# Resuming the pieces of GLA, S5 and mLSTM heads by stated waiting times, in an order pinned on TensorE and DVE

## The chip, the cores and the metric

The kernel runs on one core of a Trainium2 chip. The metric is device time in microseconds, from the start of an execution to its end; 0.2% of it is 3.5 us. The engines are TensorE (PE, with its weight loads as PEld), VectorE (DVE), ScalarE (ACT), GpSimd (POOL) and SyncE (SP), which issues the DMAs. Each works through its own queue in order and waits on semaphores.

## The reference

One layer of a hybrid model on a sequence of 1024 positions with 1024 channels: a mixer of three branches (512 channels each), then a feed-forward block with a convolution, each between two RMS norms. Cut to the mixer's inner parts, which the change touches:

```python
z = u @ w_in                          # u = rms_norm(x); queries, keys, values, gates of all branches
# GLA, 4 heads of 128: decay by log_sigmoid gates, in 16 chunks of 64
b = cumsum(log_a); q_dec = q * exp(b); k_inv = k * exp(-b)
kv = einsum(k * exp(b_last - b), v);  state = dec * state + kv       # over the chunks
o = q_dec @ s_prev + tril(q_dec @ k_inv.T) @ v;  o = rms_norm(o) * silu(r)
# S5, 32 groups of 16 channels, 64 complex states each
x[t] = ab * x[t-1] + bb @ u[t];  y = Re(c @ x) + d * u
# mLSTM, 4 heads of 128: conv + silu on q and k, stabilised gates, in 16 chunks of 64
c_new = sc * c + (w * k).T @ v;  qk = (q @ k.T) * exp(log_w - m)
hid = (s_inter * q @ c_prev + qk @ v) / max(abs(den), exp(-m));  hid = sigmoid(o) * hid
```

The rest of the layer (gates of the branches, their projections, `w_out`, the feed-forward block) is the same before and after.

## The kernel before, in words

All matmuls of weights run on fp32 values that are split into a high and a low part, three products for each step of 128 rows: high by high, high by low, low by high. `split` makes the two parts (ACT copies the high one at L88, DVE subtracts at L89). The first phase of the kernel, up to about 640 us, computes `z`. `chan_major` gives 128 channels for all positions in 48 matmuls of 512 columns (L126) into a PSUM tile `z` of two banks; `tok_mm` gives 128 positions for 256 channels in 24 matmuls (L184). There are two such `z` tiles, three single banks `m` (`bank`), and one bank `q` (`bank2`) for S5. In SBUF the S5 work has nine buffers of 128x512 (`q4`), the GLA and mLSTM work has fourteen of 128x1024 (`g`).

Beside these projections, on the same TensorE, run the pieces of the three branches. They are Python generators, and a `yield` ends a piece:

- `gla_gates` (one z tile, L332; then L337 to L356 on DVE and ACT) makes the decays of a head; `gla_inner` does the head: transposes of the decayed keys (L368), masked scores (L374, L375), chunk products (L384) and the decay chain of the states on DVE (L394, 15 steps), values (L400), the read-out (L410, added at L412), squares on POOL (L413), the norm (L415 to L417) and transposes out (L423, L425). The main program multiplies the decays by the projections at L890, L891 and L894.
- `s5_set`, eight times after `s5_base`: the set's input and its tables on POOL (L723 to L727, L735 to L737), two transposes (L742, L746), the response `kt` (L752, L753) which eight DMAs turn into the Toeplitz tile `tt`; the angles of the rotation through POOL, DVE and ACT (L767, L768, sine at L773, L774, cosine L776); `bv` times `ut` (L781); the rotation on DVE (L789) with eight scans (L799); then `ut` times `tt` (L812, copied out by ACT at L813), the states times `ca` (L816, added at L818), and, after every second set, transposes of `y` (L825).
- `ml_gates` and `ml_inner`: transposes of the keys (L552), scores (L559), states (L568, L571), read-out (L579 to L592), transposes out (L597). Convolution and SiLU of q and k (`conv_silu2`) are ACT L525, three DVE L527, ACT L530, DVE L531.

The list `running` holds the open generators; `advance()` steps each of them by one piece. It is called after a whole `chan_major` and after every fourth `tok_mm`; in the GLA and mLSTM loops `midway` also steps the S5 generator in the middle of a `chan_major`, six times in ten. This is the order in which the program is written. A scheduler then sets each engine's queue: among the instructions that are ready by its own cost model it takes the earliest written.

Of the kernel before, what the change touches and what calls it, by code (L numbers as in the profile page):

```python
# [32 lines left out]
def hybrid_layer(ctx: ExitStack, tc: tile.TileContext, a, out, dbg=None):  # L33
# [53 lines left out]
    def split(hi, lo, src):  # L87
        return (ordered("act", act.copy(hi, src)),  # L88
                ordered("dve", dve.tensor_tensor(lo, src, hi.bitcast(F32), op=ALU.subtract)))  # L89

# [26 lines left out]
    def chan_major(wt, i, xh, xl, ps=None, ns=(0, 1)):  # L117
# [14 lines left out]
    midway = []  # L132
# [7 lines left out]
    RATE = 0.6  # L140
# [38 lines left out]
    def tok_mm(wt, i, lhs, put, c0, to=None):  # L179
        hi, lo = wt  # L180
        ps = big()[:, 0, 0:hi.shape[2]] if to is None else to([128, hi.shape[2]])
        for k in range(8):
            for p, (l, r) in enumerate(((0, hi), (1, hi), (0, lo))):
                pe.matmul(ps, lhs(l, k, i), r[:, k, :],  # L184
                          start=(k == 0 and p == 0), stop=(k == 7 and p == 2))
        put(i, c0, ps)

# [141 lines left out]
    def gla_gates(h):  # L329
        ps = big()  # L330
        for n in range(2):
            pe.matmul(ps[:, n, :], wg[:, h * 128:(h + 1) * 128], lrx[:, n * 512:(n + 1) * 512],  # L332
                      start=True, stop=True)
        z = flat(ps)
        bias = cols[:, 40 + h:41 + h]
        ax, mn, b = g([128, S]), g([128, S]), g([128, S])
        dve.tensor_scalar(mn, z, bias, 0.0, op0=ALU.add, op1=ALU.min)  # L337
        dve.scalar_tensor_tensor(out=ax, in0=mn, scalar=2.0, in1=z, op0=ALU.mult, op1=ALU.subtract)
# [12 lines left out]
        return ax, b, mn, dec  # L351
# [7 lines left out]
    def gla_inner(h, E, r2):  # L359
        qd, ki, kd, dec = E  # L360
        vt = g([128, 8, 128])
        sync.dma_start(vt, v_dram[0][:, :, h * 128:(h + 1) * 128].rearrange("i p e -> p i e"))
        kt = g([128, 8, 128])
        for hf in range(2):
# [4 lines left out]
            act.copy(kt[:, hf * 4:hf * 4 + 4, :], ps)  # L369
        for hf in range(2):  # L370
# [5 lines left out]
        yield  # L376
        st = [g([128, 8, 128]) for _ in range(2)]
        pool.memset(st[0][:, 0, :], 0.0)
        for o in range(2):
# [22 lines left out]
        yield  # L402
        yield
        for hf in range(2):
# [8 lines left out]
            pool.tensor_tensor(sq, oo, oo, op=ALU.mult)  # L413
            ssq = small.tile([128, 4], F32, tag="ssq4", name="ssq4")
            dve.tensor_reduce(ssq, sq, axis=AX.X, op=ALU.add)  # L415
            rs = rstd_of(ssq, 4, DH)
            dve.tensor_tensor(oo, oo, rs.unsqueeze(2).to_broadcast([128, 4, 128]), op=ALU.mult)  # L417
        yield
        yield
# [24 lines left out]
    def ml_gates():  # L444
# [21 lines left out]
        yield  # L466
# [9 lines left out]
        yield  # L476
# [6 lines left out]
        yield  # L483
# [12 lines left out]
        yield  # L496
# [10 lines left out]
        yield  # L507
# [35 lines left out]
    def ml_inner(h, wm, qm, km, tm):  # L543
# [4 lines left out]
        for e in range(2):  # L548
            ps = bank([128, 4, 128])
            for q in range(4):  # L550
# [3 lines left out]
                              kwx[:, h, e * 4:e * 4 + 4].unsqueeze(2).to_broadcast([128, 4, 128]), op=ALU.mult)  # L554
        for e in range(2):
# [6 lines left out]
        yield  # L562
# [10 lines left out]
        yield  # L573
        nn = g([128, 8, 129])
        for j0, n in ((0, 3), (3, 3), (6, 2)):
# [8 lines left out]
            dve.tensor_tensor(dst, dst, pa[:, 0:n, :], op=ALU.add)  # L584
        rd = small.tile([128, 8], F32, tag="rd", name="rd")
# [7 lines left out]
        yield  # L593
        for e in range(2):
# [4 lines left out]
            dve.scalar_tensor_tensor(out=tm[0][:, t], in0=tm[0][:, t], scalar=1.0,  # L599
                                     in1=po.rearrange("p a b -> p (a b)"), op0=ALU.add, op1=ALU.mult)  # L600
        sync.dma_start(o_dram[2][h], tm[0])
# [99 lines left out]

    def s5_set(s):
# [11 lines left out]
        bst = s5p.tile([128, 2, 4, 16], F32, tag="bst", name="bst", bufs=1)  # L714
        for i, nm, p0 in ((0, "s5_b_re", 0), (0, "s5_b_im", 64), (1, "s5_b_im", 0), (1, "s5_b_re", 64)):
            sync.dma_start(bst[p0:p0 + 64, i], a[nm][0, gs].rearrange("g p h -> p g h"))
        cl = s5p.tile([64, 3, 64], F32, tag="cl", name="cl", bufs=1)
        for i, nm in ((0, "s5_c_re"), (1, "s5_c_im"), (2, "s5_c_re")):
            sync.dma_start(cl[:, i, :], a[nm][0, gs].rearrange("g h p -> (g h) p"))
# [7 lines left out]
        pool.tensor_copy(zr_, zt.rearrange("p j (g h) -> p g j h", h=16)[:, :, ::-1, :])  # L727
        ps = bank2([128, 2, 64])
# [9 lines left out]
        yield  # L738
# [8 lines left out]
        act.copy(ut, ps)  # L747
        kt = s5p.tile([16, 4, 15, 16], F32, tag="kt", name="kt", bufs=1)
# [28 lines left out]
        yield  # L777
# [26 lines left out]
        yield  # L804
        yield
        if s % 2 == 0:
            ysp.append(s5p.tile([128, 8, 128], F32, tag="ys", name="ys", bufs=1))
        ys = ysp[-1]
        dst = ys[:, :, c0:c0 + 64].rearrange("p j (g h) -> p g j h", h=16)
        ps = bank2(sq_)  # L810
        for q in range(4):
            pe.matmul(ps[:, q, :], ut[:, q, :], tt[:, q, :], start=True, stop=True)  # L812
        act.copy(dst, ps.rearrange("p q (j h) -> p q j h", h=16))  # L813
# [5 lines left out]
        if s % 2 == 0:  # L819
            return  # L820
        yield
        for e in range(2):
            ps = bank2(sq_)
            for q in range(4):
                pe.transpose(ps[:, q, :], ys[:, e * 4 + q, :], ident)  # L825
            yt = q4(sq_)
            act.activation(yt, ps, AF.Gelu_apprx_tanh)
            sync.dma_start(y_dram[s // 2][:, e * 512:(e + 1) * 512], yt.rearrange("p a b -> p (a b)"))

    ysp = []  # L830

    def s5_all():
        s5_base()
        yield
        for s in range(8):
            while s // 4 not in su_done:
                yield
            yield from s5_set(s)
            yield

    running = []
    credit = [0.0]

    def advance():
# [732 lines left out]
```

## Time and profile before

| | |
|---|---|
| median of 3 runs | 1745.9 us (1744.11 to 1747.18) |
| profiled execution, time | 1745.36 us |
| its span | 1743.6 us, so 1.76 us lie around it |
| granted TensorE clock, mean | 0.994 |
| PE, PEld busy | 1689.5 us (97%), 1412.1 us (81%) |
| DVE, ACT, POOL busy | 1151.8 us (66%), 646.8 us (37%), 398.1 us (23%) |

The span runs from the first to the last instruction. Busy shares are means over stages with different limits, and matmuls are pipelined, so the mean length of a matmul in a group is longer than the distance between two starts. A wait is the idle time in front of an instruction, put down to the engine and line whose semaphore came last. An idle engine matters only where TensorE waits for it in the end.

### The profile page before, as it was taken

Reading aid. Unit: us, or ns where it says so; the run is one execution under the profiler, and the core shown is the slowest. Engines: PE = TensorE matmul, PEld = TensorE weight load, DVE = VectorE, ACT = ScalarE, POOL = GpSimd, SP = SyncE. Lnnn points to the kernel's source line nnn. Section 1 sums busy time; section 2 is a strip of 40 time slices with the busy share of each in tenths; the row PEclk is TensorE's granted clock in tenths of the full one; section 3 lists DMA queues with packets and bytes.
Section 4 is the critical chain, followed back from the end, with each engine's and each line's share of the span. In section 5 each row is a group of like instructions: output and inputs, shape, how many; then the busy total and the mean of one; then the engine's idle time right before and its main releaser. Section 6 shows DMA issues by size and latency. Waiting matters only on the chain. (4 is left out here: it accounts for less than half of the span.)

```text
span 1743.6 us, 21877 instructions
## 1 busy us (share of the span) xinstructions
PE 1689.5 (97%) x8556; PEld 1412.1 (81%) x8556; DVE 1151.8 (66%) x1462; ACT 646.8 (37%) x940; POOL 398.1 (23%) x437
## 2 busy tenths in 40 slices
PE   6999998999999999999899999999999999999997
PEld 6997877897888888888688788788888888888886
DVE  4426677536667675444745654967777787669987
ACT  4544533333443223333510233433333333344343
POOL 1163243333334012222000011022322332101021
PEclk9999999999999999999899999999999999999999
DMA  6242131333141322434674643222232223483161
GB/s 205 68 113 60 43 88 34 92 91 89 23 133 49 97 85 85 127 115 145 222 249 144 217 142 125 73 73 82 76 90 79 85 73 97 169 283 127 55 218 54
DMA packets 196440, 195.10 MB, mean 112 GB/s; under 512 B 29208, under 2 KB 154305, under 8 KB 196337
## 3 DMA queue, kind: packets, MB, share of 16 engines
q1 hardware_dynamic: 195456, 190.56, 34.9%
q0 software_dynamic: 880, 3.15, 0.5%
q8 instruction: 67, 1.10, 0.3%
q14 instruction: 37, 0.30, 0.1%
HBM read 143.32 MB, written 48.25 MB: 110 GB/s over the span
## 5 line engine op out<-in xcount | busy, mean ns | idle before, releaser
L89 DVE TENSOR_TENSOR lo<-raw,hi 128x512 fp32r<-128x512 f32 (+3 forms) x163 | 174.7, 1091 | 132.0 <-ACT hi L88 129.3
L88 ACT CAST hi<-raw 128x512 fp32r<-128x512 f32 (+3 forms) x163 | 130.2, 833 | 283.1 <-PE z L126 122.0
L983 POOL TENSOR_TENSOR raw<-raw 128x512 f32<-128x512 f32 x28 | 39.5, 1412 | 472.4 <-DVE lo L89 472.4
L126 PE MATMUL z<-ohl,hi 128*128 128x512 f32 x448 | 123.3, 398 | 6.1 <-ACT ohl L1098 6.1
L126 PEld LDWEIGHTS z<-ohl,hi 128*128 128x128 f32 x448 | 85.5, 191 | 26.1 <-ACT ohl L1098 6.5
L68 POOL TENSOR_SCALAR rstd<-ssq 128x1 f32<-128x1 f32 (+1 forms) x32 | 9.3, 292 | 316.4 <-ACT x L1262 262.5
L126 PE MATMUL z<-u0h,hi 128*128 128x512 f32 x240 | 79.5, 408 | 1.4 <-DVE g L894 1.4
L126 PE MATMUL z<-u0h,lo 128*128 128x512 f32 x240 | 77.0, 398 | 0.0
L126 PE MATMUL z<-u0l,hi 128*128 128x512 f32 x240 | 76.5, 398 | 0.0
L126 PE MATMUL z<-u1h,hi 128*128 128x512 f32 x240 | 75.4, 395 | 0.0
L126 PE MATMUL z<-u1h,lo 128*128 128x512 f32 x240 | 75.0, 392 | 0.0
L126 PE MATMUL z<-u1l,hi 128*128 128x512 f32 x240 | 74.9, 393 | 0.0
L126 PE MATMUL z<-ohl,lo 128*128 128x512 f32 x224 | 70.2, 396 | 0.0
L1303 DVE SCALAR_TENSOR_TENSOR cv<-u,fcol,cv 128x1023 f32<-128x1023 f32 (+1 forms) x38 | 48.7, 1280 | 23.9 <-ACT cv L1301 23.9
L89 DVE TENSOR_TENSOR xl<-raw,xh 128x512 fp32r<-128x512 f32 x57 | 51.8, 935 | 11.2 <-ACT xh L88 8.3
L1301 ACT ACTIVATE cv<-u,fcol 128x1024 f32<-128x1024 f32 x19 | 23.6, 1244 | 89.9 <-DVE u L1001 89.9
L789 DVE TENSOR_TENSOR q<-q,q 128x512 f32<-128x512 f32 x72 | 49.5, 714 | 8.7 <-PE q L812 8.3
L126 PEld LDWEIGHTS z<-u0h,lo 128*128 128x128 f32 x240 | 45.3, 190 | 9.7 <-issue 0.2
L126 PEld LDWEIGHTS z<-u1h,lo 128*128 128x128 f32 x240 | 45.1, 188 | 9.8
L126 PEld LDWEIGHTS z<-u1l,hi 128*128 128x128 f32 x240 | 44.9, 188 | 9.9 <-issue 0.2
L126 PEld LDWEIGHTS z<-u0l,hi 128*128 128x128 f32 x240 | 44.8, 189 | 9.6 <-issue 0.4
L126 PEld LDWEIGHTS z<-u1h,hi 128*128 128x128 f32 x240 | 44.5, 188 | 9.3
(561 smaller groups left out, 5006.0 us busy)
## 6 DMA issues: line engine op xcount, KB each, us to landing
raw<-in_w_in_dram SPq DMA_DIRECT2D x48, 512.0 KB, 5.3
pt<-gate SPq DMA_DIRECT2D x24, 512.0 KB, 3.3
raw<-in_ffn_w_up_dram SPq DMA_DIRECT2D x22, 512.0 KB, 4.0
raw<-in_ffn_w_gate_dram SPq DMA_DIRECT2D x22, 512.0 KB, 5.3
h<-cv SPq DMA_DIRECT2D x21, 512.0 KB, 2.6
bx<-in_ffn_w_down_dram SPq DMA_DIRECT2D x15, 512.0 KB, 4.4
by<-in_ffn_w_down_dram SPq DMA_DIRECT2D x15, 512.0 KB, 5.1
gate<-u SPq DMA_DIRECT2D x11, 512.0 KB, 3.0
```

What stands on the lines that cost most here:

```text
L68: pool.tensor_scalar(r, ssq, 1.0 / width, EPS, op0=ALU.mult, op1=ALU.add)
L88: return (ordered("act", act.copy(hi, src)), ordered("dve", dve.tensor_tensor(lo, src, hi.bitcast(F32), op=ALU.subtract)))
L89: ordered("dve", dve.tensor_tensor(lo, src, hi.bitcast(F32), op=ALU.subtract)))
L126: pe.matmul(ps[:, n, :], l[:, k, c], r(k, n), start=(k == 0 and p == 0), stop=(k == nk - 1 and p == 2))
L789: dve.tensor_tensor(o, x, y, op=op)
L983: pool.tensor_tensor(a22, a21, a22, op=ALU.add)
L1301: first = act.activation(cv, src, AF.Identity, scale=fcol[:, 44 + f:45 + f], bias=fcol[:, 66 + f:67 + f])
L1303: ins = dve.scalar_tensor_tensor(out=cv[:, k:], in0=src[:, 0:S - k], scalar=fcol[:, (2 - k) * 22 + f:(2 - k) * 22 + f + 1], in1=cv[:, k:], ...
```

## The change

`advance`, `midway`, `extra` and `pump` go. In their place stands a list `turns` of generators with a due time each. `tick` is called after every six matmuls of `chan_major` (with 1.37 us, two halves) and halfway and at the end of each `tok_mm` (with 1.45 us each); it adds its time to a clock of the program and resumes the one generator that is longest overdue. A generator yields the time that it wants to wait before its next piece. `note` adds, at each resumption, a dependency without a semaphore from the first TensorE and the first DVE instruction of the piece to the newest instruction written before on that engine (splits of weights excepted), so that the scheduler can't put the piece ahead of it.

Beside this: `gla_gates` is a generator with two `m` banks in halves of 512 columns, no longer one z tile; the squares go from POOL to ACT; the product `ut` times `tt` stands before `bv` times `ut`; `s5_load` issues the loads of the next set after the rotation; the transposes of `y` are a generator of their own; `s5_all` starts ahead of the S5 input; `ml_inner` starts with the keys' convolution and takes q and o from a list when they are there.

```diff
-            if k == 3 and midway:
-                midway[0]()
+            tick(6 * len(ns) * 0.114)
...
+    def note(first=None):
+        traced = nc.cur_bb.bb.instructions
+        bound, work = set(), 0.0
+        for ins in traced[seen[0]:]:
+            e = ins.engine
+            if e == mybir.EngineType.PE:
+                work += 0.13
+            if e not in (mybir.EngineType.PE, mybir.EngineType.DVE):
+                continue
+            if first is not None and e not in bound and e in newest:
+                bound.add(e)
+                tc.add_manual_dep(ins, newest[e],
+                                  mybir.DependencyInfo(mybir.DependencyClass.NoSync, mybir.DependencyReason.DATA),
+                                  reason="turn")
+            if ins.name not in free_:
+                newest[e] = ins.name
...
+    def resume(turn_):
+        note()
+        try:
+            wait = next(turn_[1])
+        except StopIteration:
+            turns.remove(turn_)
+            wait = 0.0
+        now[0] += note(turn_)
+        turn_[0] = now[0] + wait
...
+    def tick(us):
+        now[0] += us
+        due = [t for t in turns if t[0] <= now[0]]
+        if due:
+            resume(min(due, key=lambda t: t[0]))
...
-        ps = big()
-        for n in range(2):
-            pe.matmul(ps[:, n, :], wg[:, h * 128:(h + 1) * 128], lrx[:, n * 512:(n + 1) * 512],
+        for n in range(2):
+            t = slice(n * 512, (n + 1) * 512)
+            z = bank([128, 512])
+            pe.matmul(z, wg[:, h * 128:(h + 1) * 128], lrx[:, t], start=True, stop=True)
...
-            pool.tensor_tensor(sq, oo, oo, op=ALU.mult)
+            act.activation(sq, oo, AF.Square)
+        yield 2.5
...
-        yield
+        yield 8.0
+        if s % 2 == 0:
+            ysp.append(s5p.tile([128, 8, 128], F32, tag="ys", name="ys", bufs=1))
...
+            pe.matmul(ps[:, q, :], ut[:, q, :], tt[:, q, :], start=True, stop=True)
+        act.copy(dst, ps.rearrange("p q (j h) -> p q j h", h=16))
+        yield 1.5
...
+        if s < 7:
+            s5_in.append(s5_load(s + 1))
+        yield 16.0
...
-        km = conv_silu2(ps, 4 + h)
+        of = []
+        spawn(ml_inner(h, wm, conv_silu2(ps, 4 + h), of), 6.0)
```

The lines move with it: L332 to L381, L368 to L415, L374 to L422, L375 to L423, L394 to L442, L410 to L459, L412 to L461, L413 to L462, L425 to L480, L552 to L607, L568 to L628, L767, L768, L776 to L842, L843, L851, L753 to L828, L773, L774 to L848, L849, L781 to L865, L789 to L873, L799 to L883, L812 to L859, L813 to L860, L816 to L893, L742 to L816, L746 to L820, L825 to L903, L890, L891, L894 to L940, L941, L943, L525, L527, L530, L531 to L580, L582, L585, L586, L126 to L128.

Three places show what the order becomes. The first is TensorE at the S5 set that runs beside GLA head 1's gates. Before, `ut` times `tt` (L812) stands behind `bv` times `ut` (L781), a whole projection later:

```order
L126 MATMUL z_2142<-u1h_113,hi_1702 128x512 x2
L126 MATMUL z_2142<-u1l_114,hi_1702 128x512 x2
L126 MATMUL z_2142<-u1h_113,lo_1703 128x512 x2
L812 MATMUL q_2191<-q4_1952,q4_1924 128x128 x4
L410 MATMUL m_2203<-g_1977,g_959 64x128 x7
L410 MATMUL m_2220<-g_1978,g_959 64x128 x8
L368 MATMUL m_2240<-ident_72,g_1719 128x128 x4
```

After, it is L859 and stands ahead of L865 (`bv` times `ut`):

```order
L128 MATMUL z_1910<-u1h_113,lo_1749 128x512 x2
L859 MATMUL q_2033<-q4_1946,q4_1864 128x128 x4
L128 MATMUL z_1910<-u1h_113,hi_1748 128x512 x2
L128 MATMUL z_1910<-u1l_114,hi_1748 128x512 x2
L128 MATMUL z_1910<-u1h_113,lo_1749 128x512 x2
L128 MATMUL z_2047<-u0h_111,hi_1748 128x512 x2
L128 MATMUL z_2047<-u0l_112,hi_1748 128x512 x2
L128 MATMUL z_2047<-u0h_111,lo_1749 128x512 x2
L865 MATMUL q_2056<-q4_1864,q4_1863 128x128 x4
```

Six main matmuls that end one projection and six of the next lie between the two S5 products, and the read-out L410 that followed L812 stands elsewhere.

The second place is DVE in the same set, at the angles of the rotation (L767, L768, L776 before) and the decay chain of GLA head 0 (L394):

```order
L394 SCALAR_TENSOR_TENSOR g_1977<-g_1977,dec_970 128x128 x6
L767 TENSOR_SCALAR q4_1963<-q4_1961 128x512
L394 SCALAR_TENSOR_TENSOR g_1977<-g_1977,dec_970 128x128
L768 TENSOR_SCALAR q4_1963<-q4_1963 128x512
L394 SCALAR_TENSOR_TENSOR g_1978<-g_1977,dec_970,g_1978 128x128
L394 SCALAR_TENSOR_TENSOR g_1978<-g_1978,dec_970 128x128 x3
L767 TENSOR_SCALAR q4_1963<-q4_1961 128x512
L394 SCALAR_TENSOR_TENSOR g_1978<-g_1978,dec_970 128x128
L768 TENSOR_SCALAR q4_1963<-q4_1963 128x512
L394 SCALAR_TENSOR_TENSOR g_1978<-g_1978,dec_970 128x128 x3
L776 TENSOR_SCALAR q4_1963<-q4_1963 128x512
L894 SCALAR_TENSOR_TENSOR g_1718<-z_2035,g_1718 128x1024
```

After, with L842, L843 and L851 for the angles, L442 for the decay chain, and L940, L941 for the products of the decays with the next projection:

```order
L842 TENSOR_SCALAR q4_1957<-q4_1955 128x512
L843 TENSOR_SCALAR q4_1957<-q4_1957 128x512
L842 TENSOR_SCALAR q4_1957<-q4_1955 128x512
L843 TENSOR_SCALAR q4_1957<-q4_1957 128x512
L851 TENSOR_SCALAR q4_1957<-q4_1957 128x512
L442 SCALAR_TENSOR_TENSOR g_1884<-g_1884,dec_1148 128x128 x5
L940 TENSOR_TENSOR g_1822<-z_1910,g_1822 128x1024
L442 SCALAR_TENSOR_TENSOR g_1884<-g_1884,dec_1148 128x128
L941 TENSOR_TENSOR g_1821<-z_1910,g_1821 128x1024
L442 SCALAR_TENSOR_TENSOR g_1884<-g_1884,dec_1148 128x128
L873 TENSOR_TENSOR q4_2064<-q4_2054,q4_1957 128x512
```

The angles now stand in one block, and the last seven steps of the decay chain behind it, with L940 and L941 between them.

The third place is TensorE at the first mLSTM head. Before, the transposes of the keys (L552) stand behind the last matmul of the q projection:

```order
L126 MATMUL z_4002<-u1l_114,hi_3989 128x512 x2
L126 MATMUL z_4002<-u1h_113,lo_3990 128x512 x2
L552 MATMUL m_4232<-ident_72,g_3911 128x128 x4
L816 MATMUL q_3974<-q4_3593,q4_3878 128x128 x4
L552 MATMUL m_4238<-ident_72,g_3911 128x128 x3
L126 MATMUL z_4093<-u0h_111,hi_3996 128x512 x2
```

After, L607 stands inside the q projection (`z_4026`), between two halves of an S5 product (L859):

```order
L128 MATMUL z_4026<-u1l_114,hi_3898 128x512 x2
L128 MATMUL z_4026<-u1h_113,lo_3899 128x512 x2
L859 MATMUL q_4079<-q4_3987,q4_3941 128x128 x2
L607 MATMUL m_4061<-ident_72,g_4019 128x128 x4
L607 MATMUL m_4067<-ident_72,g_4019 128x128 x4
L859 MATMUL q_4079<-q4_3987,q4_3941 128x128 x2
L128 MATMUL z_4026<-u1h_113,hi_3898 128x512 x2
L128 MATMUL z_4026<-u1l_114,hi_3898 128x512 x2
```

Twelve matmuls of the 48 of the q projection are still to come behind it.

## Rows read from the trace of the kernel before

**Rows 1.** Stretches: us; busy us of PE, PEld, DVE, ACT, POOL; granted clock; DMA.

```profile
62.00:640.00 578.00, 556.61 (x3461) 479.62 (x3460) 361.58 (x566) 231.44 (x339) 186.75 (x219) 0.99 0.28 78
...
298.40:301.80 3.40, 3.40 (x11) 2.80 (x11) 3.22 (x7) 0.00 (x0) 0.91 (x2) 0.51 0.21 19
```

**Rows 2.** TensorE's waits, 62-640 us (last row 0-62): us in total, times, longest.

```profile
PE q L816 <- DVE q L789: 7.4, 5, 3.2
PE m L368 <- DVE g L412: 3.5, 2, 2.8
PE m L580 <- DVE g L582: 1.9, 3, 0.7
PE z L184 <- DVE g L356: 1.6, 1, 1.6
PE q L816 <- POOL rstd L68: 1.5, 1, 1.5
PE z L126 <- DVE g L894: 1.4, 1, 1.4
...
PE m L498 <- DVE g L495: 1.1, 1, 1.1
...
PE q L825 <- ACT q L827: 0.3, 1, 0.3
...
PE q L635 <- DMA q<-in_s_a_re_dram: 0.8, 1, 0.8
```

**Rows 3.** Timeline of TensorE at full clock: start us, us, instruction.

```profile
302.33 0.62 PE L126 MATMUL z<-u0l,hi 128*128 128x512 f32 x2
302.79 0.39 PE L126 MATMUL z<-u0h,lo 128*128 128x512 f32 x1
```

**Rows 4.** Timelines of TensorE (L753) and DVE, two S5 sets [idle before].

```profile
185.42 0.35 PE L753 MATMUL q<-q,q 128*16 128x112 f32 x2
...
185.25 1.90 DVE L394 SCALAR_TENSOR_TENSOR g<-g,dec 128x128 f32<-128x128 f32 x5 [1.11 <-ACT g L389]
188.33 1.25 DVE L767 TENSOR_SCALAR q<-q 128x512 f32<-128x512 f32 x1 [1.18 <-POOL q L604]
...
198.33 0.65 DVE L776 TENSOR_SCALAR q<-q 128x512 f32<-128x512 f32 x1 [1.90 <-POOL q L604]
...
254.99 0.35 PE L753 MATMUL q<-q,q 128*16 128x112 f32 x2
...
269.87 0.42 DVE L776 TENSOR_SCALAR q<-q 128x512 f32<-128x512 f32 x1
```

**Rows 5.** DVE by form, 62-640 us: count | busy us, mean ns | idle before.

```profile
L789 DVE TENSOR_TENSOR q<-q,q 128x512 f32<-128x512 f32 x72 | 49.5, 714 | 8.7 <-PE q L812 8.3
...
L89 DVE TENSOR_TENSOR lo<-raw,hi 128x2048 fp32r<-128x2048 f32 x16 | 37.6, 2353 | 13.8 <-ACT hi L88 13.8
...
L799 DVE TENSOR_TENSOR_SCAN q<-r,q 128x128 f32<-128x128 f32 x64 | 21.8, 412 | 0.0
...
L531 DVE SCALAR_TENSOR_TENSOR g<-g 128x1024 f32<-128x1024 f32 x8 | 10.2, 1280 | 6.4 <-ACT g L530 6.4
...
L527 DVE SCALAR_TENSOR_TENSOR g<-z,cols,g 128x1023 f32<-128x1023 f32 x8 | 10.2, 1276 | 0.6 <-ACT g L525 0.6
...
L890 DVE TENSOR_TENSOR g<-z,g 128x1024 f32<-128x1024 f32 x4 | 4.9, 1225 | 18.7 <-PE z L126 18.7
```

**Rows 6.** Groups of ACT by form, 62 to 640 us, columns as before.

```profile
L525 ACT ACTIVATE g<-z,cols 128x1024 f32<-128x1024 f32 x8 | 9.7, 1212 | 1.7 <-PE z L126 1.7
...
L530 ACT ACTIVATE g<-g 128x1024 f32<-128x1024 f32 x8 | 8.5, 1061 | 31.8 <-DVE g L527 31.7
...
L530 ACT ACT_TABLE_LOAD x4 | 5.1, 1283 | 7.8 <-DVE g L527 7.8
...
L813 ACT COPY ys<-q 128x512 f32<-128x512 f32 x8 | 4.7, 582 | 15.3 <-PE q L812 15.3
```

**Rows 7.** DMA issues, 62 to 640 us, with the median landing time.

```profile
q<-kt SPq DMA_DIRECT2D x64, 32.0 KB, 2.0
```

More of the change, by code (lines that the diff above doesn't have):

```diff
@@ L87, in split @@
     def split(hi, lo, src):
-        return (ordered("act", act.copy(hi, src)),
+        made = (ordered("act", act.copy(hi, src)),
                 ordered("dve", dve.tensor_tensor(lo, src, hi.bitcast(F32), op=ALU.subtract)))
+        free_.update(i.ins.name for i in made)
+        return made
     def load_w(srcs, rows, cols, late=None, keep=None):
@@ L127, in chan_major, with spawn, finish_turn @@
                               start=(k == 0 and p == 0), stop=(k == nk - 1 and p == 2))
-            if k == 3 and midway:
-                midway[0]()
-        return ps
-    midway = []
+            tick(6 * len(ns) * 0.114)
+        return ps
+    now, turns, seen, newest, free_ = [0.0], [], [0], {}, set()
+    def note(first=None):
[14 more added lines that the diff above has]
+                newest[e] = ins.name
+        seen[0] = len(traced)
+        return work
+    def resume(turn_):
[7 more added lines that the diff above has]
+        turn_[0] = now[0] + wait
+    def spawn(gen, wait=0.0):
+        turns.append([now[0] + wait, gen])
+        return turns[-1]
+    def tick(us):
[3 more added lines that the diff above has]
+            resume(min(due, key=lambda t: t[0]))
+    def finish_turn(turn_):
+        while any(t is turn_ for t in turns):
+            resume(turn_)
     def flat(ps):
@@ L412, in gla_inner @@
             dve.tensor_tensor(oo, oo, pb, op=ALU.add)
-            pool.tensor_tensor(sq, oo, oo, op=ALU.mult)
+            act.activation(sq, oo, AF.Square)
+        yield 2.5
+        for hf in range(2):
             ssq = small.tile([128, 4], F32, tag="ssq4", name="ssq4")
[L415 to L419, printed above, removed]
+            dve.tensor_reduce(ssq, os_[hf][:, 1], axis=AX.X, op=ALU.add)
+            sums.append(rstd_of(ssq, 4, DH))
+        yield 6.0
+        for hf in range(2):
+            oo = os_[hf][:, 0]
+            dve.tensor_tensor(oo, oo, sums[hf].unsqueeze(2).to_broadcast([128, 4, 128]), op=ALU.mult)
+        yield 3.0
+        while r2[0] is None:
+            yield 1.0
         for hf in range(2):
@@ L776, in s5_set @@
         dve.tensor_scalar(cs, cs, -2.0, 1.0, op0=ALU.mult, op1=ALU.add)
-        yield
+        yield 8.0
+        if s % 2 == 0:
+            ysp.append(s5p.tile([128, 8, 128], F32, tag="ys", name="ys", bufs=1))
+        ys = ysp[-1]
+        dst = ys[:, :, c0:c0 + 64].rearrange("p j (g h) -> p g j h", h=16)
+        ps = bank2(sq_)
+        for q in range(4):
+            pe.matmul(ps[:, q, :], ut[:, q, :], tt[:, q, :], start=True, stop=True)
+        act.copy(dst, ps.rearrange("p q (j h) -> p q j h", h=16))
+        yield 1.5
         vv, ww = q4(sq_), q4(sq_)
@@ L833, in s5_all, with su_half @@
         s5_base()
-        yield
+        yield 20.0
         for s in range(8):
             while s // 4 not in su_done:
-                yield
+                yield 2.0
             yield from s5_set(s)
[L839 to L844, printed above, removed]
-        step([gen for gen in running])
-    def extra():
-        credit[0] += RATE
-        if credit[0] >= 1.0 and s5 in running:
-            credit[0] -= 1.0
-            step([s5])
-    def step(gens):
-        for gen in gens:
-            try:
-                next(gen)
-            except StopIteration:
-                running.remove(gen)
-    def pump(n):
-        for _ in range(n):
-            advance()
-    def su_half(hf, mid=None):
+    def su_half(hf):
         wt = wide_tile(w_in, C_SU + hf * 256, 256)
@@ L867, in su_half @@
             tok_mm(wt, i, tok_lhs, put_dram(su_dram), hf * 256, bank)
-            if i % 4 == 3:
-                advance()
-            if i == 1 and mid:
-                mid()
+            if i == 1 and hf == 0:
+                gates.append(spawn(gla_gates(0, E)))
+                spawn(ml_gates(), 10.0)
         su_done.append(hf)
@@ L888, in hybrid_layer @@
         pk = flat(chan_major(wt, 0, u_hi, u_lo))
-        advance()
+        finish_turn(gates.pop(0))
         dve.tensor_tensor(E[1], pk, E[1], op=ALU.mult)
@@ L1043, in put_gate @@
         return ins
-    midway.clear()
     xs = (u_hi, u_lo)
```

130 lines of the change are left out of this document (65 added, 65 removed).

## The prediction

> **What bounds the kernel now.** I read the waits of TensorE first, for the stretch from 62 to 640 us, because the code behind that stretch keeps its order: after it the two programs issue the same instructions. Then the busy times of the same stretch, then the timelines of TensorE, DVE around single stalls, last the groups of instructions by form for prices.
>
> In that stretch TensorE is busy 556.6 of 578.0 us [rows 1]. DVE works 361.6 us, ACT 231.4, POOL 186.8, so no other engine is a bound by its sum; what can be won is TensorE's idle time. The list of waits names it: 7.4 us of the S5 product L816 for DVE's rotation L789, 3.5 us of the transposes L368 for L412, 1.9 us L580 for L582, 1.6 us L184 for L356, 1.5 us again L816, 1.4 us L126 for L894, and five smaller from 1.1 to 0.3 us that make 3.4, in all 20.7 us [rows 2]. A wait of 0.8 us for an S5 load stands ahead of the stretch [rows 2]. To this come two slow stretches of the clock. [...] Each costs 3.4 x (1 - 0.51) = 1.7 us, and over the whole stretch the clock is 0.99, so there are no more of them [rows 1]. The ceiling of the gain is 20.7 + 0.8 + 3.4 = **24.9 us**, 1.4% of the run.
>
> **The change, part by part.** TensorE's instructions stay the same in number and kind; main matmuls and pieces only change places. A switch between them costs what a 128x512 matmul costs anyway, 0.23 us start to start [rows 3]. So the sum is: stalls that go, less stalls that come.
>
> *What goes.* L816 stands for xx from the rotation, and L812 (`ut` times `tt`) stood just ahead of it in the queue, so the buffers of `ut` and `tt` came free late and the rotation, which needs them, began late: DVE's L789 was idle 8.7 us, 8.3 of it for L812 [rows 5]. The change puts that product (now L859) ahead of `bv` times `ut` (L865), and the product with xx (L893) 16 us and more of TensorE's work behind L865. The rotation needs 9 x 0.71 + 8 x 0.41 = 9.7 us of DVE by [rows 5], with other work between. I take 7.4 + 1.5 and the 0.7 us of L812 as gone: 9.6. The gates of the next GLA head no longer take a z buffer, which ends the two waits for z, 1.6 + 1.4 = 3.0. The groups of the mLSTM read-out now lie apart: 1.9. L368 no longer follows L412 on a crowded DVE: 3.5. The S5 base is issued earlier: 0.8. The rest of the small ones is 2.7, and with no idle of 2.8 us left at the old places the two clock drops go too: 3.4. That is all 24.9; I give the old places nothing back, since every one of them is re-ordered.
>
> *What comes.* The waiting times that the pieces now state are numbers in the code, and the order on TensorE and DVE is pinned to them, so a piece that is late on the chip holds what is queued behind it. The trace of before tells how late. From the end of the last matmul of the S5 response (L753, 185.77 us) to the end of L776 on DVE (198.98) the chain over ACT, POOL and DVE takes 13.2 us in the set shown, of which 10.7 from L767 on are links through POOL and ACT [rows 4]; in the next set, from 255.34 to 270.29, it takes 14.9 [rows 4]. After the change DVE has L842, L843, L842, L843, L851 of this chain in one block, with nothing between in that set where before the decay steps L394 filled the gaps. What stands behind L851 waits for the chain:
>
> - GLA head 0: the second half of L459 needs the last decay step L442. Behind L851 stand 5 steps at 0.38 [rows 4], two products of the decays with the projection at 1.22 [rows 5] and two more steps: 13.2 + 1.9 + 1.2 + 0.4 + 1.2 + 0.4 = 18.3 us after the last L828. On TensorE it stands 15.9 us after it (matmuls counted in the order at 0.23 and 0.11). Stall 2.4, with 14.9 for the chain 4.1, and none where the chain is 2.4 shorter. The wait of L865 for its bank adds 0.8: 3.2.
> - GLA head 1: the first half of L422 stands 26.3 us after L828 and wants a bank that L461 frees behind the whole rotation: 13.2 + 9.7 + L943 1.2 + L89 2.35 + three operations of 0.71 = 28.6, so 2.3; the small ones around it (L820, L903, L865, the other half) 2.4. Together 4.7.
> - GLA head 2: L865 stands 11.9 us after L828, and its bank is freed by ACT's L860, which stands behind L462, whose operand comes from an L461 behind L851: 13.2 + 0.71 + two of 0.58 [rows 6] = 15.1, stall 3.2. Then the second half of L422, 22.6 + 3.2 = 25.8 us after L828, wants the bank that the first L480 frees. Behind L851 stand ahead of it five operations of 0.71, L943, L89, eight L873 and eight L883, 3.6 + 1.2 + 2.35 + 5.7 + 3.3 = 16.1, so it ends at 13.2 + 16.1 + 0.7 = 30.0: stall 4.2. Together 7.4.
> - Head 3 and the mLSTM values, by the same subtraction: 1.3.
> - mLSTM: the first transposes of a head, L607, stand 36 of the 48 matmuls of the next projection behind the k projection, 36 x 0.23 = 8.3 us. Before, the same L552 stood behind all 48. The convolution and SiLU take 1.21 + 3 x 1.28 + 1.28 for a table load + 1.06 + 1.28 = 8.7 us [rows 5, 6] and the hand-overs between engines. In the first head ACT has the sine of an S5 set, which waits for POOL, ahead of the SiLU. I take 4 us there and 1 in each of the other three, and 3 us for the third bank that L628 wants behind the rotation: 10. The bounds are 0 (no table load, nothing ahead of the SiLU on ACT, the rotation done) and 16 (4 in each head).
>
> Sum of what comes: 3.2 + 4.7 + 7.4 + 1.3 + 10 = **26.6 us**, bounded below by about 12 (only the largest stall of each S5 set, since a stall gives everything behind it time, and 1 us for each mLSTM head) and above by 40 (three heads like head 2, four mLSTM heads at 4, one clock drop).
>
> *What I cost at nothing.* The gates in halves give DVE 8 more instructions and about 1 us (two halves of 0.71 for one of 1.22); DVE is 37% idle there. The squares that go from POOL to ACT add 8 x 0.6 us to an engine that is 60% idle; without that cover they would cost at most these 4.8 us. The seven loads of the next S5 set are issued behind the rotation instead of at the set's start: SP waits for data, not for its queue, and these loads come earlier than they are wanted. The eight transfers that turn `kt` into `tt` land 2.0 us after issue (median) [rows 7], well before L859, 8.9 us behind L828.
>
> Forecast: 1745.4 - 24.9 + 26.6 = **1747.1 us** for a run like the profiled one (1745.36, with a span of 1743.6), which is 0.5 below the median shown. I round to 1747.
>
> **Rivals.**
> *The stated times hold* (B). For it: four of the five new stalls hang on one late instruction, L851, and TensorE's own delay at the first one lets DVE catch up. Then about 12 us come and 24.9 go: 1732.5, between 1725 and 1740. Against it: the lag of 13.2 and 14.9 us is measured, and no instruction of that chain is made faster.
> *DVE's pinned queue falls behind* (C), the slower end. Place: DVE behind L851 in the sets beside the GLA heads. It decides where L851 ends 14.9 us or more after the last L828 in every set: then decay, masks, z and splits of weights (L89) all come behind it and the stalls of head 2 repeat. 3 x 7.4 + 4 x 4 + one clock drop 1.7 = 39.9, so 1745.4 - 24.9 + 39.9 = 1760.4, between 1755 and 1766. For it: the L789 already ends TensorE's longest waits [rows 2]. Against: DVE has 216 us of idle time in the stretch.
> *The clock swings* (D). In the trace a clock drop follows only the idles of 2.8 and 3.2 us, and the waits of up to 1.6 us [rows 2] left the clock where it was. Should many short idles drop it too, then 12 places with a new stall would each cost 1.7 us: 1747 + 20 = 1767. [...]
> That the pins have no effect can be left out, since the order of both programs shows the pieces moved.
>
> **How the numbers follow.** Chances: the forecast (A) 0.38, B 0.35, C 0.23, D 0.04. A's own range is 1741 to 1754: the new stalls at 20 to 33 us. A measurement of this kernel tells 0.2%, 3.5 us, from no change. Of A, 0.05 lies below 1742.4, 0.20 within and 0.13 above 1749.4; of B 0.34 below and 0.01 within; of C and D 0.25 above and 0.02 within. So faster 0.39, same 0.23, slower 0.38. The range 1729 to 1762 leaves out some 0.07 of B below and 0.13 of C and D above.
>
> **What would show it.** Right: L893 waits for DVE under 2 us in all, no waits for z by L402 or L943; new waits of L459, L865 and L422 for DVE and ACT beside the GLA heads of 2 to 4 us each, and of L607 for L586 in all four mLSTM heads; TensorE's busy time in the stretch unchanged within 2 us. Wrong: new waits under 12 us in all (then B), or waits of L459, L422 and L607 over 40 us with a granted clock of 0.98 or less in the stretch (C, D). A time after 640 us that differs by more than 2 us would make the whole frame wrong.

## The result and the profile after

The changed kernel takes 1787.4 us (median of 4 runs, 1785.4 to 1789.9) against 1746.5 us for the kernel before (4 runs): a ratio of 1.0234, 95% interval [1.0214, 1.0254]. That is 41 us slower, outside the range of 1729 to 1762 us. The profiled execution spans 1788.2 us against 1743.6.

The loss lies in the first phase, as two things of about equal size. These are busy times of TensorE, PEld, DVE, ACT and POOL in stretches of the changed kernel, then the granted clock and the DMA share (columns as in [rows 1]); the last row is one of the slow stretches of the clock:

```profile
0.00:62.00 62.00, 45.94 (x318) 43.40 (x319) 23.55 (x30) 25.75 (x54) 11.91 (x41) 0.94 0.50 154
62.00:690.00 628.00, 585.67 (x3526) 502.81 (x3525) 376.59 (x594) 240.16 (x354) 182.56 (x214) 0.97 0.26 73
690.00:1788.20 1098.20, 1078.43 (x4716) 881.97 (x4714) 753.97 (x846) 384.30 (x539) 204.77 (x175) 0.99 0.39 127
340.00:346.80 6.80, 5.39 (x17) 4.26 (x18) 4.25 (x7) 0.00 (x0) 4.83 (x4) 0.50 0.26 48
```

TensorE's waits from 62 to 690 us (us in total, times, longest; two of 0.5 us are left out), which answer to [rows 2]:

```profile
PE q L804 <- DVE ys L895: 6.5, 5, 2.8
PE q L865 <- ACT ys L860: 6.3, 5, 3.0
PE m L619 <- DVE g L586: 5.3, 2, 3.3
PE m L607 <- DVE g L586: 5.1, 1, 5.1
PE m L422 <- DVE g L480: 4.0, 1, 4.0
PE m L478 <- DVE g L471: 3.5, 2, 2.8
PE z L128 <- DVE g L582: 2.8, 1, 2.8
PE q L820 <- ACT dec L394: 2.6, 1, 2.6
PE m L523 <- DVE g L520: 2.4, 1, 2.4
PE m L640 <- DVE g L620: 1.4, 1, 1.4
PE m L662 <- DVE g L608: 1.3, 1, 1.3
```

With the two left out they make 42.2 us, where the kernel before has 20.7 [rows 2]: 21.5 us more. The other half is the clock. Up to 690 us the changed kernel has ten stretches at half of the full clock (0.50 granted, as in the last row above), 47.6 us together (six of 3.4 us and four of 6.8); the kernel before has two, 6.8 us (granted 0.52 and 0.51). That is 40.8 us more, but 5.4 us more of them lie inside idle times and cost nothing there, so by estimate they cost some 35.4 x (1 - 0.50) = 18 us. With 1.4 us more of waits before 62 us and 2.4 after 690 the account is 21.5 + 18 + 1.4 + 2.4 = 43 us, and the spans differ by 44.6; some 1.5 us are not accounted for.

In the changed kernel every slow stretch up to 690 us goes with an idle time of TensorE. Of the eleven idles from 2.3 to 5.1 us up to 700 us (the wait for the first matmul is left out), ten have one that begins before the idle ends or within about 1 us behind it. In the kernel before, those of 2.8 and 3.2 us have one, and one of 2.4 us at the start has none.

Three of the stalls, row by row. First TensorE and DVE around L804, the first transposes of the next S5 set, which need the `q` bank that L895 reads (start us, us, instruction, then the idle time and who ended it):

```profile
222.98 0.63 PE L128 MATMUL z<-u1l,hi 128*128 128x512 f32 x2
226.41 0.34 PE L804 MATMUL q<-ident,cl 64*128 64x64 f32 x2 [2.80 <-DVE ys L895]
...
229.71 1.05 PE L128 MATMUL z<-u1l,hi 128*128 128x512 f32 x2
```

```profile
221.26 0.69 DVE L471 TENSOR_TENSOR g<-g,rstd 128x512 f32<-128x512 f32 x1 [0.65 <-POOL rstd L69]
221.87 2.28 DVE L89 TENSOR_TENSOR lo<-raw,hi 128x2048 fp32r<-128x2048 f32 x1
225.06 0.69 DVE L471 TENSOR_TENSOR g<-g,rstd 128x512 f32<-128x512 f32 x1 [0.91 <-POOL rstd L69]
225.67 0.68 DVE L895 TENSOR_TENSOR ys<-ys,q 128x512 f32<-128x512 f32 x1
```

TensorE stops at 223.6 with the product L893 done. DVE first does a weight split (L89), then L471, which waits 0.91 us for POOL's norm, and only then L895. L804 starts 2.8 us late, and behind it a pair of main matmuls takes 1.05 us where it took 0.63 ahead of the idle (granted clock 0.50 from 227.4 to 230.8 us).

Second L478, the transposes of the last GLA head's read-out, with DVE:

```profile
388.56 1.12 PE L478 MATMUL m<-ident,g 128*128 128x128 f32 x4 [2.77 <-DVE g L471]
```

```profile
375.60 1.25 DVE L842 TENSOR_SCALAR q<-q 128x512 f32<-128x512 f32 x1 [4.27 <-POOL q L669]
...
384.92 0.43 DVE L851 TENSOR_SCALAR q<-q 128x512 f32<-128x512 f32 x1 [3.87 <-POOL q L669]
385.26 1.27 DVE L466 TENSOR_REDUCE ssq<-g 128x4 f32<-128x512 f32 x2
387.81 0.69 DVE L471 TENSOR_TENSOR g<-g,rstd 128x512 f32<-128x512 f32 x1 [1.28 <-POOL rstd L69]
```

The norm (L466, L471) stands behind the whole block of the S5 angles, L842 to L851, and DVE idles 4.3 us for POOL ahead of it and 3.9 us at its last link.

Third the first L607, with ACT and DVE:

```profile
437.75 0.61 PE L859 MATMUL q<-q,q 128*128 128x128 f32 x4
443.44 1.97 PE L607 MATMUL m<-ident,g 128*128 128x128 f32 x8 [5.07 <-DVE g L586]
```

```profile
438.52 0.72 ACT L848 ACTIVATE q<-q,sgnpi 128x512 f32<-128x512 f32 x1 [7.52 <-POOL g L600]
...
439.77 1.28 ACT L585 ACT_TABLE_LOAD   x1
441.07 1.06 ACT L585 ACTIVATE g<-g 128x1024 f32<-128x1024 f32 x1
```

```profile
442.16 1.22 DVE L586 SCALAR_TENSOR_TENSOR g<-g 128x1024 f32<-128x1024 f32 x1 [0.60 <-ACT g L585]
```

ACT's queue has the sine of the S5 set (L848) ahead of the SiLU, and L848 waits for POOL, so the SiLU (table load, L585, L586) ends at 443.4 us and L607 is 5.1 us late.

The chain of the S5 angles, which the prediction took as the late link, takes about as long as before. For the set that answers to [rows 4], end of the last L828 and then DVE:

```profile
186.84 0.35 PE L828 MATMUL q<-q,q 128*16 128x112 f32 x2
```

```profile
194.23 0.42 DVE L842 TENSOR_SCALAR q<-q 128x512 f32<-128x512 f32 x1
...
202.70 0.43 DVE L851 TENSOR_SCALAR q<-q 128x512 f32<-128x512 f32 x1 [3.86 <-POOL q L870]
```

It runs from 187.19 to 203.13, 15.9 us, where the kernel before has 13.2 for this set; over all eight sets it takes 11.8 to 15.9 us, 13.4 in the mean, before 12.4 to 14.9, 13.2 in the mean.

### The profile page after: what moved, and what is told of

The parts are those of the page before. It is cut to its first block, busy times and chain, and to the rows that moved or that the text cites. A ratio compares the mean times of both kernels' runs of the same rounds, so it can differ in the third digit from the quotient of the medians.

```text
span 1788.2 us, 21876 instructions
## 1 busy us (share of the span) xinstructions
PE 1710.0 (96%) x8556; PEld 1428.2 (80%) x8556; DVE 1154.1 (65%) x1470; ACT 650.2 (36%) x947; POOL 399.2 (22%) x429
## 5 line engine op out<-in xcount | busy, mean ns | idle before, releaser
L89 DVE TENSOR_TENSOR lo<-raw,hi 128x512 fp32r<-128x512 f32 (+3 forms) x163 | 174.7, 1091 | 133.4 <-ACT hi L88 130.7
L128 PE MATMUL z<-ohl,hi 128*128 128x512 f32 x448 | 123.1, 397 | 5.6 <-ACT ohl L1140 5.0
L128 PEld LDWEIGHTS z<-ohl,hi 128*128 128x128 f32 x448 | 85.0, 191 | 25.7 <-ACT ohl L1140 5.4
L128 PE MATMUL z<-u0h,hi 128*128 128x512 f32 x240 | 79.1, 409 | 2.8 <-DVE g L582 2.8
L128 PE MATMUL z<-u1h,hi 128*128 128x512 f32 x240 | 81.2, 418 | 0.0
L128 PE MATMUL z<-u1h,lo 128*128 128x512 f32 x240 | 77.8, 404 | 0.0
L128 PE MATMUL z<-u1l,hi 128*128 128x512 f32 x240 | 77.0, 401 | 0.0
L128 PE MATMUL z<-u0h,lo 128*128 128x512 f32 x240 | 75.9, 396 | 0.0
L128 PE MATMUL z<-u0l,hi 128*128 128x512 f32 x240 | 75.5, 395 | 0.0
L128 PE MATMUL z<-ohl,lo 128*128 128x512 f32 x224 | 70.0, 395 | 0.0
L89 DVE TENSOR_TENSOR xl<-raw,xh 128x512 fp32r<-128x512 f32 x57 | 51.8, 935 | 11.1 <-ACT xh L88 8.3
L873 DVE TENSOR_TENSOR q<-q,q 128x512 f32<-128x512 f32 x72 | 50.9, 741 | 8.0 <-ACT q L866 6.6
L128 PEld LDWEIGHTS z<-u1l,hi 128*128 128x128 f32 x240 | 46.2, 193 | 10.3
L128 PEld LDWEIGHTS z<-u1h,lo 128*128 128x128 f32 x240 | 46.2, 194 | 10.1
L128 PEld LDWEIGHTS z<-u0l,hi 128*128 128x128 f32 x240 | 45.3, 189 | 10.0
L128 PEld LDWEIGHTS z<-u0h,lo 128*128 128x128 f32 x240 | 45.2, 189 | 10.1
L128 PEld LDWEIGHTS z<-u0h,hi 128*128 128x128 f32 x240 | 42.7, 190 | 11.6 <-issue 4.1
```

The source lines that it names most:

```text
L128: pe.matmul(ps[:, n, :], l[:, k, c], r(k, n), start=(k == 0 and p == 0), stop=(k == nk - 1 and p == 2))
L873: dve.tensor_tensor(o, x, y, op=op)
```

## The experiments

Theory 1 was that DVE's pinned order makes the stalls, theory 2 that the stated waiting times do (with the pins idle), and theory A that the fall of the clock is a price of its own beside each wait, against B, that it comes from the small pieces.

| kernel | time, us | ratio to before, 95% | waits 62 to 690 us | slow clock to 690 us | up to the GLU + from it on, us |
|---|---|---|---|---|---|
| before | 1746.5 | 1 | 20.7 | 6.8 | 828.6 + 915.0 |
| changed | 1787.4 | 1.0234 [1.0214, 1.0254] | 42.2 | 47.6 | 872.5 + 915.7 |
| no pins | 1766.8 | 1.0108 [1.0084, 1.0133] | 33.0 | 30.6 | 852.3 + 912.9 |
| pins on TensorE alone | 1768.3 | 1.0131 [1.0114, 1.0149] | 33.8 | 27.2 | 854.1 + 911.9 |
| S5 waits longer | 1768.6 | 1.0120 [1.0087, 1.0152] | 30.5 | 30.6 | 856.5 + 905.1 |
| mLSTM waits longer | 1774.7 | 1.0155 [1.0117, 1.0194] | 36.7 | 34.0 | 861.4 + 906.2 |
| longer waits, no pins | 1739.4 | 0.9968 [0.9952, 0.9984] | 15.5 | 6.8 | 826.3 + 909.0 |
| longer waits, pins | 1758.2 | 1.0057 [1.0036, 1.0078] | 26.1 | 20.4 | 845.7 + 908.4 |
| and fifth set later, no pins | 1748.8 | 0.9993 [0.9978, 1.0009] | 19.0 | 10.2 | 832.9 + 906.9 |
| before, S5 products swapped | 1759.3 | 1.0079 [1.0062, 1.0096] | 24.6 | 34.0 | 845.3 + 912.8 |
| swapped, states' product later | 1761.0 | 1.0075 [1.0062, 1.0088] | 29.0 | 20.4 | 848.3 + 912.1 |
| changed, zero matmuls (third) | 1782.0 | 1.0183 [1.0165, 1.0202] | 32.0 | 27.2 | 866.5 + 914.0 |

Waits, slow clock and the last column are of one profiled execution each; the wait of L1041 (1.4 and 1.1 us), which in the two kernels without DVE's pins and with the short waiting times falls ahead of 690 us, is left out. Each ratio is to the kernel before as it was measured alongside, 1746.5 to 1748.2 us. The last column splits the span at the first matmul of the S5 branch's GLU, a projection well behind the first phase (the wait in front of it counts to the second part); in every kernel 3928 matmuls stand from it on.

The longer waiting times change more than the stalls. While a piece is still open, the main program computes the branch gates' projections in 96 matmuls a pair, later in 84. Pieces that end later keep it longer in the first form: TensorE has 24 matmuls more (some 5.5 us at 0.23) with the longer S5 waits, with the fifth set later and with the states' product later, and 12 more with the longer mLSTM waits and in both kernels with all the longer waits. And the first matmul of the GLU waits (before, then changed):

```profile
PE z L126 <- ACT ohl L1098: 6.1, 1, 6.1
PE z L128 <- ACT ohl L1140: 5.0, 1, 5.0
```

This wait stands, with a slow stretch close to it, in every profile but those of the five kernels with longer waiting times and of the first one with zero matmuls. What takes it away was not tested. So of the gain of the longer S5 and mLSTM waits in the profiled executions 16.0 and 11.1 us lie ahead of the GLU, and 10.6 and 9.5 us behind it, where none of the stalls above stands.

**Without the pins.**

```diff
-            if first is not None and e not in bound and e in newest:
+            if False and first is not None and e not in bound and e in newest:
```

> The dependencies without a semaphore are left out, everything else is as in the changed kernel. Theory 1 (the pins hold DVE's queue behind L851 and so make the stalls): TensorE's waits between 62 and 660 us fall from 42 us to under 30 and the time to 1770 us or less. Theory 2 (the due times set where the pieces are written, the scheduler keeps nearly that order by itself, and they are too short for the chip): waits 38 to 46 us, time 1782 to 1792 us.

1766.8 us: the pins cost 20.6 us. The time is that of theory 1, though its waits are 33 us and not under 30, and TensorE's order hardly changes. Both theories are in it: half of the loss stays without pins. The longest waits that are left:

```profile
PE m L607 <- DVE g L586: 5.1, 1, 5.1
PE q L865 <- ACT ys L860: 4.4, 4, 2.2
PE q L804 <- DVE ys L895: 4.3, 5, 2.7
PE m L619 <- DVE g L586: 4.2, 2, 2.9
```

L478 and L820, 6.1 us in the changed kernel, are not in that list any more; L607 stays at 5.1, and L449 is new with 2.0.

**On which engine.**

```diff
-            if first is not None and e not in bound and e in newest:
+            if first is not None and e == mybir.EngineType.PE and e not in bound and e in newest:
```

> The dependencies stay on TensorE and are left out on DVE alone. Theory 1 (DVE's pins cost the 20 us that leaving all pins out brought back): 1764 to 1770 us, waits of TensorE 31 to 36 us between 62 and 690 us, as without any. Rival (TensorE's pins cost them): 1784 to 1790 us and 42 us of waits, as in the changed kernel.

1768.3 us, as without any. TensorE's pins alone cost nothing, so it is DVE's, set beside them, that cost the 20 us. L478, shown above, has no wait here (start us, us), and on DVE the norm now stands ahead of the angles:

```profile
380.16 1.03 PE L478 MATMUL m<-ident,g 128*128 128x128 f32 x8
```

```profile
364.23 1.47 DVE L466 TENSOR_REDUCE ssq<-g 128x4 f32<-128x512 f32 x2
366.33 0.69 DVE L471 TENSOR_TENSOR g<-g,rstd 128x512 f32<-128x512 f32 x1 [0.64 <-POOL rstd L69]
...
370.17 1.25 DVE L842 TENSOR_SCALAR q<-q 128x512 f32<-128x512 f32 x1 [1.18 <-POOL q L669]
...
379.47 0.65 DVE L851 TENSOR_SCALAR q<-q 128x512 f32<-128x512 f32 x1 [3.85 <-POOL q L669]
```

L466 and L471 run while POOL makes the first products of the angles, and L842 comes behind them.

**S5 pieces later.**

```diff
-        yield 1.5
+        yield 5.0
...
-        if s == 0:
-            yield 6.0
+        yield 6.0
```

> S5 pieces only: the wait stated between L859 and L865 goes from 1.5 to 5.0 us, and every set, not only the first, waits 6.0 us before L804. Theory 2: the waits of L865 for L860 (6.3 us) and of L804 for L895 (6.5 us) go, with the clock drops at 149, 227 and 538 us (1.7 us each), so 1787 - 12.8 - 5.1 = 1769 us. Theory 1 (DVE's queue is late whatever is stated): waits move to other lines, time within 5 us of 1787. Theory 3 (the price is the clock, which falls by the density of small pieces and not by single idles): the drops stay as many, 1775 us or more.

1768.6 us (1763.3 to 1773.9, the profiled execution 1763.3), the time of theory 2, but only in part for its reason: 10.6 us of the gain in the profile lie behind the GLU. L865 for L860 falls from 6.3 to 0.3 us and L804 is out of the list; of the drops at 149, 227 and 538 us none is left at its place.

**mLSTM pieces later.**

```diff
-        spawn(ml_inner(h, wm, conv_silu2(ps, 4 + h), of), 6.0)
+        spawn(ml_inner(h, wm, conv_silu2(ps, 4 + h), of), 12.0)
...
-        yield 6.0
+        yield 10.0
         qm = of[0]
```

> mLSTM pieces only: the head starts 12 us after its keys' convolution is issued instead of 6, the scores 10 us after q is there instead of 6. Theory 2: the waits of L607 (5.1 us) and L619 (5.3 us) go, with the clock drops at 442 us (3.4 us) and 575 us (1.7 us): 1787 - 10.4 - 5.1 = 1772 us. Theory 1: waits move to L628, L639 and the z tiles, within 5 us of 1787.

1774.7 us (1769.3 to 1780.6, the profiled execution 1769.3), 2.7 above the number of theory 2, and here too 9.5 us of the gain in the profile lie behind the GLU. L607 is out of the list, L619 at 0.7 us; L865 is up by 1.4.

**All at once.** The three edits together, and the first wait of the mLSTM gates from 5.0 to 8.0.

> All three at once: no pins, the S5 waits longer (5.0 after L859, 6.0 before every L804), the mLSTM waits longer (12 and 10), and the first wait of the mLSTM gates 8 instead of 5. If what the three brought back singly (20.6, 18.7 and 12.6 us) is from different stalls, it adds up: 1787 - 52 = 1735 us, faster than the kernel before. If they are the same stalls seen three times: 1755 to 1765 us.

1739.4 us: 48 of the 52 us add up. Ahead of the GLU, where the stalls are, the profiles add up as well: 20.2 + 16.0 + 11.1 = 47.3 us singly and 46.2 together. So the three causes hold different stalls in the main. The gates' longer wait was not run alone; the wait of L523, 2.4 us in the changed kernel, is gone with it. This version is 0.3% faster than the kernel before, but of the 8.3 us between the two profiled spans only 2.3 lie ahead of the GLU and 6.0 behind it, so the first phase is about as long as before. What waits are left, the largest of them:

```profile
PE z L128 <- DVE g L582: 4.4, 1, 4.4
PE z L227 <- ACT ev L241: 2.1, 2, 1.3
PE m L640 <- DVE g L642: 2.1, 2, 1.3
PE m L619 <- DVE g L586: 1.8, 1, 1.8
```

**Longer waits with the pins.** The version above with `if first is not None` back.

> The longer waits (S5, mLSTM, mLSTM gates) with the pins on both engines. If the pins only make too short waits worse: 1736 to 1744 us, as without them. If they cost by themselves what leaving them out brought back in the changed kernel: 1755 to 1762 us.

1758.2 us. The pins cost 19 us (19.4 ahead of the GLU in the profiles, 16 by the two ratios) also where the waits are longer, so they don't only make short waits worse. L478 waits 3.8 us, L640 5.0, L662 2.8, each behind DVE.

**The fifth S5 set later.**

```diff
-        yield 6.0
+        yield 20.0 if s == 4 else 6.0
```

> The version without pins and with longer waits, and the fifth S5 set waits 20 us before L804 instead of 6, so that its rotation on DVE stands behind the convolution (L582) for which TensorE waits 4.4 us there. If that wait and its clock drop of 1.7 us go: 1739 - 6 = 1733 us. If the later set pushes other waits up: 1738 us or more.

1748.8 us (12 runs from 1741.1 to 1752.3): the gain did not come, and the second expectation held. In the profiled execution (1741.9 us) the wait for L582 is gone, but L628 waits 4.5 us and L640 3.5 instead, and TensorE has 12 matmuls more than in the version with which it is compared.

**One part of the change in the kernel before.** In `s5_set` the block of `ut` times `tt` goes ahead of `bv` times `ut`:

```diff
         yield
+        ps = bank2(sq_)
+        for q in range(4):
+            pe.matmul(ps[:, q, :], ut[:, q, :], tt[:, q, :], start=True, stop=True)
+        act.copy(dst, ps.rearrange("p q (j h) -> p q j h", h=16))
         vv, ww = q4(sq_), q4(sq_)
```

> The kernel before with one part of the change: the S5 product of ut and tt stands ahead of that of bv and ut. By the prediction the waits of the states' product (L816 before) and of the product that was moved, 9.6 us, and one clock drop of 1.7 us go: 1747 - 11 = 1736 us. Rival: the moved product then waits for the eight transfers of tt or holds the q bank, and the time stays within 3.5 us of 1747.

1759.3 us, 12.5 us slower where 11 us of gain were expected. The waits of TensorE and the rotation's group on DVE (here L797, before L789):

```profile
PE q L816 <- DVE q L797: 13.5, 5, 4.6
PE q L789 <- ACT ys L785: 3.4, 3, 1.5
```

```profile
L797 DVE TENSOR_TENSOR q<-q,q 128x512 f32<-128x512 f32 x72 | 49.2, 716 | 0.7 <-ACT q L792 0.4
```

The rotation now starts in time: DVE's idle time before it is 0.7 us, where [rows 5] has 8.7. But with `ut` times `tt` ahead of it the product `bv` times `ut` (L789 here) moves back in TensorE's queue: from its end to the start of the states' product L816 the eight sets have 11.0 to 15.5 us, waits included, where the kernel before has 22.1 to 36.9. The rotation, which needs that product, has so much less time ahead of L816, and L816 waits 13.5 us.

**And the states' product one step later.** A third empty `yield` behind the rotation.

> The kernel before with the product of ut and tt first, and one more step between the rotation and the states' product (three empty steps instead of two). If the swap is worth its 9.6 us only with a later states' product: the 13.5 us of L816's waits go to under 3 and the time to 1740 us or less. If the wait moves to the next set (L742, L816 again): 1755 to 1760 us.

1761.0 us. The wait of the states' product (L817 here) falls to 3.1 us, and L184, L746 and L597 now wait 3.7, 3.3 and 2.4 us. A step of `running` moves every piece behind it by a whole projection, and TensorE has 24 matmuls more, so what the swap is worth with a later product alone was not isolated.

**Matmuls of zeros.** In the changed kernel, products with a tile of zeros are added to the open `z` tile in front of stalls:

```diff
+        for _ in range(n):
+            pe.matmul(cur[0][:, 0, :], zero[0], u_hi(0, 0), start=False, stop=False)
```

> Matmuls of a tile of zeros are added into the open z tile right before five instructions that wait 5.1, 4.0, 3.3, 3.0 and 2.8 us: 21, 17, 13, 12 and 11 of them, so TensorE works through what was idle time; the result of z does not change. Theory A (an idle of 2.4 us and more lets the clock fall, and that fall is a cost beside the wait): the five clock drops behind these places go, 3.4 + 3.4 + 1.7 + 1.7 + 1.7 = 12 us less, 1775 us. Theory B (the drops come from the pieces, not from the idle time): drops stay, 1787 to 1790 us.

> The matmuls of zeros again, in the changed kernel, with those of the scores of an mLSTM head now at the third head (13) and those of the second half of L422 split 9 and 8 around the first half, the others as before (21, 12, 11). Theory A (the fall of the clock is a price beside the wait): the drops behind these five idles go, 3.4 + 3.4 + 1.7 + 1.7 + 1.7 = 12 us, and 1775 to 1780 us. Theory B (the drops come from the small pieces, not from idle time): as many slow stretches as in the changed kernel, 47.6 us of them, and 1787 us or more.

Both take 1790.1 us (ratios 1.0237 and 1.0259). 17 and 13 of the matmuls in each did not stand at their idle times (in both another head's L422, since the second run puts all 17 ahead of one half and not 9 and 8 as its expectation says; another head's L619 in the first, and in the second one that still waits 2.8 us behind them) and, by count, cost what they take, 3.9 and 3.0 us. At the three other places the slow stretches went, so neither run decides by its time.

> The matmuls of zeros a third time, in the changed kernel, only at places where they stand right in the idle time: 12 before L865 of the first S5 set, 11 before L804 of the third, 17 before the second half of the last L422, 21 before the first L607. Theory A (an idle of this length also lets the clock fall): slow stretches of 3.4, 3.4, 6.8 and 6.8 us go and no wait gets longer, so 1787 - 10 = 1777 us. Theory B (the clock falls by the small pieces): no gain, 1785 us or more.

1782.0 us (1775.3 to 1782.8), 5.4 us less than the changed kernel: theory A, at half of its number (6.0 us in the profiles ahead of the GLU). TensorE at the first of the four places (L144 are the zeros, L891 is L865):

```profile
145.52 0.62 PE L128 MATMUL z<-u1h,lo 128*128 128x512 f32 x2
145.97 2.88 PE L144 MATMUL z<-u0h,zfill 128*128 128x512 f32 x12
149.13 1.05 PE L891 MATMUL q<-q,q 128*128 128x128 f32 x7 [0.28 <-ACT ys L884]
```

Of the idle of 2.98 us there 0.28 is left. Of the slow stretches at 149, 227, 340 and 442 us, 20.4 us, none is left (behind the third place pairs of main matmuls take 0.62 to 0.64 us from 341.1 us on, where the changed kernel has 1.05), which by estimate should be worth half of that, 10 us; one of 3.4 us at 106 us became 6.8, and L607 still waits 2.2 us behind 21 matmuls that took 4.8, so its stall is longer by 1.9.

## Why the prediction was wrong

The direction was given 0.38, but the time lies above every case, D's 1767 too. Two terms of the sum failed.

- **The sum of what comes, 26.6 us**, is 42.2 on the chip. Some of the places that were worked out came near: the second half of L422 4.0 us (predicted 4.2), the first L607 5.1 (4), L865 beside head 0 0.7 (0.8). Others did not: L865 beside head 2 waits 1.3 (3.2), the first half of L422 0.5 (2.3), L607 in the other three heads and the third bank of L628 nothing (1 each and 3), and the longest wait of L865, 3.0 in the first set, was not counted. L459 has no wait, since TensorE came to its last matmuls 20.4 us after the last L828, where 15.9 were counted at 0.23 and 0.11. And L804, L619, L478, L820, L523 and L128 for L582 make 23.1 us and were missed or counted as 2.4 of small ones. The step "what stands behind L851 waits for the chain" looked at that chain alone; L804 waits for an addition that stands on DVE behind a norm (at 226 us) or behind work of an mLSTM head (at 538), L619 for the second convolution. The longer waits, which take away L804's, L865's, L607's and most of L619's, brought back 16.0 and 11.1 us ahead of the GLU.
- **The clock.** "The two clock drops go too" was set at -3.4 us with none to come. Ten came, 47.6 us of slow stretches. Though the trace had shown that idles of 2.8 and 3.2 us are followed by one, the predicted stalls of 3.2 and 4.2 and 4 us got no such term, and rival C had one drop. Ten of the eleven idles of this length cost their time and, by estimate, up to 1.7 or 3.4 us more, half of a slow stretch of 3.4 or 6.8. Rival D (chance 0.04) had such a term at 12 places, but from many short idles, and here the ten falls stand beside single ones of 2.37 to 5.07 us; of the 18 waits in the list of [rows 2] two had a drop.
- **The pins** stood in the argument as what holds the queue, without a price. They cost some 16 to 21 us, with short and with long waits, and with the short ones it is DVE's that do.
- *What goes*: right as to the lines. The states' product (L893) waits for nothing, z waits for L356 and L894 are gone, and so are the old L368 and L580. The cause was wrong: the swap of the products did not end L816's waits by itself, since alone it makes them longer (13.5 us), and with a later states' product they fall to 3.1. That points to the stated 16 us before L893; these without the swap were not run.
- *At nothing*: the account of waits and clock leaves some 1.5 us, so the halves of the gates, the squares on ACT and the earlier loads cost little if anything; they were not tried singly.
- From the first of the products L1041 of the branch gates on (696.9 us, before 655.5) the changed kernel is 3.2 us longer, 2.4 of it waits. The frame had allowed 2, so by its own sign it does not quite hold; but 41.4 of the 44.6 us lie ahead of it.

What stays open: which of DVE's pins cost the most (L478 is one place that the rows show; a run for each kind of piece was not made), what takes away the wait for L1140 behind the first phase, and the 1.5 us that the account leaves.

## What to carry to other kernels

Count a stall of TensorE that is longer than the ones the trace shows to be harmless (in the kernel before, those up to 1.6 us) at its time and at the slow stretch that the trace shows beside such stalls; here that nearly doubled the loss, 21.5 us of waits and some 18 of slow clock. When pieces are placed by stated times, take these from the trace for every link, the drain that frees a bank and the next piece's first use of it too, and leave the order of the engine that drains the banks to what is ready: the same pieces with longer times and without pins ran 0.3% faster than the kernel before, with a first phase about as long, and with short times and pins 2.3% slower. Where a change moves work between phases, split each profile at a place behind which nothing differs before giving a gain to a cause.

## What the runs showed of the hardware

In the changed kernel, with 12, 11, 17 and 21 matmuls of zeros into the open accumulation ahead of four idle times, the four slow stretches at these places (20.4 us at 0.50) were gone, and the time fell by 5.4 us, to 1782.0. In the two other runs 30 such matmuls stood away from the idle times, at some 0.23 us each, and both took 1790.1 us.

In the profiles of the changed kernel and of the kernel before, from 20 to 700 us, each of the five idles of TensorE from 2.98 to 5.07 us has a slow stretch (granted 0.50, 3.4 or 6.8 us long) that begins before the idle ends or within 0.8 us behind it; of the nine from 2.3 to 2.9 us seven have one, within 1.1 us; of the four from 1.5 to 2.0 us none has.
